# Feed-forward, block two: the final pair of row tiles also in seven products

## The chip, the core and the metric

The kernel runs on one core of a Trainium2 chip. The metric is the device time of one execution in microseconds. Five engines work side by side: TensorE (PE; its weight loads are PEld), VectorE (DVE), ScalarE (ACT), GpSimd (POOL) and SyncE (SP), which issues most loads. Each has its own list of instructions, fixed when the program is built, and engines wait for each other and for loads by semaphores.

## The reference

One decoder layer on 256 tokens of width 2048. The change touches the feed-forward at its end alone:

```python
h = x + jnp.concatenate([gla_out, nsa_out], axis=-1) @ w_out
m = rms_norm(h, ffn_norm_g)
return h + (jax.nn.silu(m @ w_gate) * (m @ w_up)) @ w_down
```

`w_gate` and `w_up` are 2048 x 5632, `w_down` is 5632 x 2048, all float32. What comes before (gated linear attention and native sparse attention) is not touched.

## The kernel before

**Blocks.** The 5632 hidden columns are cut into eleven blocks of 512, `fb` = 0 to 10; the change is in the second, `fb` = 1, called block two here. For each block `gate_up(fb)` makes gate and up for the 256 tokens (two token tiles of 128), and `down(fb - 1)` then multiplies the hidden values of the block before by 512 rows of `w_down` and adds them to the output. So after `gate_up(1)` comes `down(0)`, in four pieces `n` of 512 output columns, 24 matmuls each.

**Pairs.** The 2048 rows of the weights are 16 row tiles of 128, taken in 8 pairs. Plainly, a pair is eight products of a 128 x 128 token tile with a 128 x 512 weight tile (two row tiles, two token tiles, gate and up). In the other way, in the manner of Strassen and Winograd, it is seven products of sums of tokens with sums of weights. Each product is three matmuls (L1179), since float32 values are split into a high and a low part: 24 matmuls plainly, 21 with seven products. `FIRST7` and `PAIRS7` say which pairs of a block go in seven products; in block two they are 0, 2, 3, 4 and 5, and 1, 6 and 7 go plainly. The order of its pairs is `ORDER1 = (0,1,2,6,3,4,5,7)`, so pair 7 is last. The sums of tokens (`forms`) of pairs 6 and 7 are made by `late_forms` while block two runs, for the blocks after it.

**Splitting.** `in_parts` makes the high part with ScalarE (a copy that rounds, L661) and the low part with VectorE (what is left, L662). A plain pair splits its raw tile of four times 512 columns (`parts_of`). A pair of seven products splits three of the four (128 x 1536) and then two sums of 128 x 1024, `s1` and `s2` (`parts_of2`). The sums of some pairs were made early in the kernel and put into memory (`SUMS`, `sum_rows`); GpSimd's queue fetches them back (`fetch_sums`, L1168). For the others VectorE makes them when they are needed (L1210 to L1212), from the raw tile.

**Buffers.** Raw tiles come from SyncE's queue (`load4`, L1138) into three buffers `fraw`; split tiles lie in four buffers `ftwo`. A buffer is written anew when its last reader is done.

**Banks.** The products of a block are added up in eight PSUM banks, `banks[1]` to `banks[8]`. In the order lists below bank 1 is `bank_4463`, bank 2 `bank_4349`, bank 3 `bank_4368`, bank 4 `bank_4385`, bank 5 `bank_4478`, bank 6 `bank_4486`, bank 7 `bank_4482` and bank 8 `bank_4397`. Seven products of a pair add into banks 1 to 7, a plain pair adds into 2, 3, 4 and 8. So after the last pair of seven products (`last7`) banks 1, 5, 6 and 7 are final. They are read there (L1237 to L1241) into `q1`, `u`, `q5u`, `q7u` and `q57u`, and in block two three things follow from this point: `turn_act(0, (1, 5))` may transpose the hidden values of block one through banks 1 and 5, and `seed(0, ...)` puts the output's first piece into banks 6 and 7 (L1291), on which `down(0)` begins. With `last7` = 5 all this is issued ahead of pair 7; after pair 7 follow banks 2, 3, 4 and 8 with the silu and the product of gate and up (L1252 to L1256).

**Order.** The code gives the order in which instructions are issued; a scheduler moves them within each engine's list when the program is built, and the lists below are what it made.

Of the kernel before, what the change touches and what calls it, by code (L numbers as in the profile page):

```python
# [37 lines left out]
def kernel(  # L38
# [986 lines left out]

    PAIRS7, FIRST7 = tuple(range(8)), {0: (0, 2, 4), 1: (0, 2, 3, 4, 5)}

    EARLY7 = (0,1,2,3,4,5)  # L1030

# [414 lines left out]
```

## Time and profile before

| | |
|---|---|
| median of 3 runs | 1099.7 us (1098.82 to 1100.81) |
| the profiled execution | 1100.68 us |
| its span, first to last instruction | 1098.9 us |
| TensorE's granted clock | 1.000 |
| the first down stage, after block two | 495.39 to 517.22 us of the span |
| weights loaded and sums written and fetched, over the span | 271.22 MB, mean 247 GB/s |

Busy time of TensorE is partly modelled, so holes in it are seen best as waits of its weight loads (PEld) and in the chain of work that ended last. "Idle before" of a row, in square brackets, names what released it.

### The profile page before, as it was taken

How to read it: one execution, taken by the hardware profiler on the slowest of the kernel's cores; microseconds unless marked ns; L12 is line 12 of the kernel's file. 1: busy time of each engine (PE TensorE's matmuls, PEld its weight loads, DVE VectorE, ACT ScalarE, POOL GpSimd, SP SyncE). 2: the span in 40 equal slices, each digit the busy share in tenths (PEclk: the TensorE clock that was granted, in tenths of full speed). 3: DMA queues.
4: the chain of work that ended last, by engine and by line, in shares of the span. 5: the costliest groups of instructions: out<-in, count | busy, mean ns of one | idle time of the engine just before them, and what ended most of it. 6: DMA issues, size and time to landing. Idle time of an engine off the chain costs nothing.

```text
span 1098.9 us, 14699 instructions
## 1 busy us (share of the span) xinstructions
PE 1092.1 (99%) x5274; PEld 899.8 (82%) x5274; DVE 993.4 (90%) x1313; ACT 755.4 (69%) x1048; POOL 79.8 (7%) x150
## 2 busy tenths in 40 slices
PE   9999999999999999999999999999999999999998
PEld 8888888987888877888878888888888888888887
DVE  5778879986899888997999999999999999999997
ACT  7755557545687587666585866768585867777785
POOL 4100001032110100100000000000000000000000
PEclk9999999999999999999999999999999999999999
DMA  7999978467877956685566657576566768677663
GB/s 278 356 371 355 378 248 296 165 226 283 307 276 253 336 183 232 226 324 172 181 231 210 213 199 252 180 253 208 209 230 205 252 216 287 212 263 235 226 230 115
DMA packets 128885, 271.22 MB, mean 247 GB/s; under 512 B 7126, under 2 KB 9210, under 8 KB 128812
## 3 DMA queue, kind: packets, MB, share of 16 engines
q1 hardware_dynamic: 115532, 223.68, 59.2%
q0 software_dynamic: 12672, 46.14, 11.4%
q8 instruction: 41, 0.67, 0.2%
q10 hardware_dynamic: 608, 0.47, 0.1%
q14 instruction: 32, 0.26, 0.1%
HBM read 247.19 MB, written 23.07 MB: 246 GB/s over the span
## 4 chain that ended last, share of the span: by engine, by line
PE 82%; DVE 8%; issue 4%; ACT 3%; POOL 2%; DMA 1%; SPq 0%; DVEq 0%; POOLq 0%; ACTq 0%
PE bank L297 39%; PE bank L1179 36%; PE bank L215 2%; PE bank L1320 2%; DVE lo L145 2%; DVE ftwo L662 1%; DMA g<-in_x_dram 1%; PE bank L977 1%; ACT hi L144 1%; POOL sm L218 1%; DMA fraw<-in_w_up_dram 1%; ACT g L912 1%; DVE g L1111 0%; DVE g L1210 0%; POOL sc L218 0%
## 5 line engine op out<-in xcount | busy, mean ns | idle before, releaser
L1179 PE MATMUL bank<-ftwo,g 128*128 128x512 f32 x1842 | 431.3, 393 | 0.5 <-ACT ftwo L661 0.2
L1179 PEld LDWEIGHTS bank<-ftwo,g 128*128 128x128 f32 x1842 | 341.0, 188 | 77.9 <-DVE ftwo L662 5.0
L297 PE MATMUL bank<-hi,g 128*128 128x512 f32 (+1 forms) x1088 | 320.9, 376 | 0.4 <-ACT g L912 0.4
L662 DVE TENSOR_TENSOR ftwo<-fraw,ftwo 128x1536 fp32r<-128x1536 f32 (+1 forms) x130 | 256.6, 1976 | 8.2 <-ACT ftwo L661 7.4
L661 ACT ACTIVATE ftwo<-fraw 128x1536 fp32r<-128x1536 f32 (+1 forms) x130 | 216.0, 1664 | 28.3 <-DMA fraw<-in_w_up_dram 18.6
L297 PE MATMUL bank<-ftwo,g 128*128 128x512 f32 x960 | 220.6, 390 | 0.0
L297 PEld LDWEIGHTS bank<-hi,g 128*128 128x128 f32 x1088 | 191.6, 188 | 30.9 <-issue 1.0
L297 PEld LDWEIGHTS bank<-ftwo,g 128*128 128x128 f32 x960 | 179.6, 188 | 38.4 <-ACT bank L1291 0.3
L297 PE MATMUL bank<-lo,g 128*128 128x512 f32 (+3 forms) x544 | 193.0, 375 | 0.1
L144 ACT ACTIVATE hi<-raw 128x1024 fp32r<-128x1024 f32 (+3 forms) x124 | 130.7, 1059 | 81.9 <-PE bank L297 62.7
L145 DVE TENSOR_TENSOR lo<-raw,hi 128x1024 fp32r<-128x1024 f32 (+3 forms) x124 | 150.2, 1218 | 33.5 <-ACT hi L144 32.9
L661 ACT ACTIVATE ftwo<-g 128x1024 fp32r<-128x1024 f32 x76 | 80.3, 1057 | 75.1 <-DVE g L1210 48.9
L297 PEld LDWEIGHTS bank<-lo,g 128*128 128x128 f32 x544 | 98.3, 189 | 14.6 <-DVE lo L145 0.3
L662 DVE TENSOR_TENSOR ftwo<-g,ftwo 128x1024 fp32r<-128x1024 f32 x76 | 92.7, 1220 | 10.5 <-ACT ftwo L661 10.5
L662 DVE TENSOR_TENSOR ftwo<-fsum,ftwo 128x1024 fp32r<-128x1024 f32 x76 | 92.6, 1219 | 0.5 <-ACT ftwo L661 0.5
L661 ACT ACTIVATE ftwo<-fsum 128x1024 fp32r<-128x1024 f32 x76 | 79.6, 1048 | 5.4 <-DVE fsum L1212 3.7
L1303 ACT COPY g<-bank 128x512 f32<-128x512 f32 x80 | 46.0, 589 | 38.3 <-PE bank L297 36.7
L1210 DVE TENSOR_TENSOR g<-fraw 128x1024 f32<-128x1024 f32 x54 | 65.2, 1219 | 0.8 <-DMA fraw<-in_w_up_dram 0.8
L1291 ACT COPY bank<-g 128x512 f32<-128x512 f32 x80 | 45.3, 594 | 15.0 <-DVE f L1240 8.4
L661 ACT ACTIVATE g<-bank 128x512 fp32r<-128x512 f32 x46 | 27.2, 598 | 30.2 <-PE bank L215 24.3
L1168 POOL DMA_DIRECT2D g<-sums x20 | 10.6, 533 | 502.0 <-DVE ftwo L662 473.4
L215 PE MATMUL bank<-ident,g 128*128 128x128 f32 (+3 forms) x232 | 42.8, 278 | 1.3 <-DVE g L863 0.9
(250 smaller groups left out, 918.5 us busy)
## 6 DMA issues: line engine op xcount, KB each, us to landing
fraw<-in_w_gate_dram SPq DMA_DIRECT2D x86, 512.0 KB, 3.9
fraw<-in_w_down_dram SPq DMA_DIRECT2D x42, 1024.0 KB, 5.0
raw<-in_w_in_dram SPq DMA_DIRECT2D x36, 1024.0 KB, 5.8
fraw<-in_w_up_dram SPq DMA_DIRECT2D x66, 512.0 KB, 4.8
sums<-g POOLq DMA_DIRECT2D x40, 512.0 KB, 6.5
raw<-in_w_out_dram SPq DMA_DIRECT2D x16, 1024.0 KB, 8.6
g<-in_w_gate_dram SPq DMA_DIRECT2D x20, 512.0 KB, 8.4
g<-in_w_up_dram SPq DMA_DIRECT2D x20, 512.0 KB, 9.3
```

The lines of the kernel that those rows point to most:

```text
L144: act(h[:, i:i + n], r[:, k + i:k + i + n], AF.Copy)
L145: last["d"] = TT(o[:, i:i + n], r[:, k + i:k + i + n], f32(h[:, i:i + n]), ALU.subtract)
L215: return nc.tensor.transpose(o, i, ident[:n, :n])
L218: nc.gpsimd.tensor_tensor(o, i, mhalf[:i.shape[0], :i.shape[1]], ALU.pow)
L297: last["mm"] = mm(bk[t], a[:, k, t * P:(t + 1) * P], ws[k][m][:, off:off + w], start=(first_ and k == 0 and i == 0), stop=(end and k == 3 ...
L661: act(hi, ps, AF.Copy)
L662: last["d"] = TT(lo, ps, f32(hi), ALU.subtract)
L1179: mm(banks[q], x, m, start=todo[q] == total[q], stop=todo[q] == 1)
L1210: TT(s1, r[:, 1:3], r[:, 3:4].to_broadcast([P, 2, 512]), ALU.add)
L1291: last["seed", n] = nc.scalar.copy(banks[qs[n][t]], h_sb[n][:, t, :])
L1303: nc.scalar.copy(h_sb[n][:, t, :], bs[t])
L1320: mm(bk, u, m, start=(first and i == 0), stop=(end and i == 2), skip_group_check=onto)
```

## The change

Pair 7 joins the seven-product pairs of block two:

```diff
@@ FIRST7 @@
-    PAIRS7, FIRST7 = tuple(range(8)), {0: (0, 2, 4), 1: (0, 2, 3, 4, 5)}
+    PAIRS7, FIRST7 = tuple(range(8)), {0: (0, 2, 4), 1: (0, 2, 3, 4, 5, 7)}
```

`SUMS[1]` stays `(2, 3, 4, 5)`, so no sums of this pair lie in memory and VectorE makes them. `last7` of block two becomes 7, so the reads of banks 1, 5, 6 and 7, the transposes and the seeds are issued after pair 7, not ahead of it. Pair 7 is the last of its order and takes its products as 6, 1, 5, 7, 2, 3, 4; the scheduler puts 1, 5, 7, 2 and two matmuls of 3 first, then one of 6, one of 3, one of 4, the four transposes into bank 1, and the remaining two of 6 and of 4. No load is added or taken away, and the lists of the later blocks have the same order as before, but for a few VectorE rows of the next block's first two pairs.

On VectorE, where pair 4 of block two is split (`ftwo_4855` holds the sums of pair 3, `fraw_4876` is the raw tile of pair 4, `ftwo_4891` holds its sums, `fraw_4940` is the raw tile of pair 7), before and with the change as one difference:

```order
 L662 TENSOR_TENSOR ftwo_4855<-g_873_4802,ftwo_4855 128x1024 [waits DMASW6_49,Activation_49]
+L1210 TENSOR_TENSOR g_892_4946<-fraw_4940 128x1024 [waits DMAHW7_49,DMAHW0_49]
 L662 TENSOR_TENSOR ftwo_4879<-fraw_4876,ftwo_4879 128x1536 [waits DMAHW4_49,DMAHW3_49,Activation_49]
 L662 TENSOR_TENSOR ftwo_4891<-g_877_4836,ftwo_4891 128x1024 [waits DMASW7_49,Activation_49]
 L662 TENSOR_TENSOR ftwo_4891<-fsum_4837,ftwo_4891 128x1024 [waits DMASW5_49,Activation_49]
```

The first sum of pair 7 is new in VectorE's list, two pairs early, and it waits for both loads of that pair's raw tile.

On VectorE at the end of block two, before (`ftwo_4955` is pair 7, `ftwo_5006` and `ftwo_5041` are the first two tiles of `w_down`):

```order
L662 TENSOR_TENSOR ftwo_4955<-fraw_4952,ftwo_4955 128x2048 [waits DMAHW7_49,DMAHW0_49,Activation_49]
L662 TENSOR_TENSOR ftwo_5006<-fraw_5004,ftwo_5006 128x2048 [waits DMAHW1_49,Activation_49]
L1238 TENSOR_TENSOR f_891_4941<-bank_4486,f_890_4940 128x512 [waits PE_49,Activation_49]
L662 TENSOR_TENSOR ftwo_5041<-fraw_5039,ftwo_5041 128x2048 [waits DMAHW2_49,Activation_49]
L1239 TENSOR_TENSOR f_892_4942<-bank_4478,f_891_4941 128x512 [waits DVE_49]
L1240 TENSOR_TENSOR f_893_4943<-bank_4482,f_891_4941 128x512
L1252 TENSOR_TENSOR f_890_4940<-bank_4349,f_890_4940 128x512 [waits PE_49]
L1241 TENSOR_TENSOR f_894_4944<-bank_4478,f_893_4943 128x512 [waits DVE_49]
```

and with the change (`ftwo_4943` is the raw tile of pair 7, `ftwo_4951` its two sums, `ftwo_5013`, `ftwo_5048` and `ftwo_5079` are the first three tiles of `w_down`, `g_901` the low part of the hidden values of block one):

```order
L662 TENSOR_TENSOR ftwo_4943<-fraw_4940,ftwo_4943 128x1536 [waits Activation_49]
L1211 TENSOR_TENSOR fsum_4947<-g_892_4946,fraw_4940 128x512 [waits DVE_49]
L662 TENSOR_TENSOR ftwo_4951<-g_892_4946,ftwo_4951 128x1024 [waits Activation_49]
L1212 TENSOR_TENSOR fsum_4947<-fsum_4947,fraw_4940 128x512 [waits DVE_49]
L662 TENSOR_TENSOR ftwo_5013<-fraw_5011,ftwo_5013 128x2048 [waits DMAHW1_49,Activation_49]
L662 TENSOR_TENSOR ftwo_5048<-fraw_5046,ftwo_5048 128x2048 [waits DMAHW2_49,Activation_49]
L662 TENSOR_TENSOR ftwo_4951<-fsum_4947,ftwo_4951 128x1024 [waits Activation_49]
L662 TENSOR_TENSOR g_901_4998<-bank_4463,g_900_4997 128x4x128 [waits Activation_49]
L1238 TENSOR_TENSOR f_896_4978<-bank_4486,f_895_4977 128x512 [waits PE_49]
L662 TENSOR_TENSOR ftwo_5079<-fraw_5077,ftwo_5079 128x2048 [waits DMAHW3_49,Activation_49]
L1239 TENSOR_TENSOR f_897_4979<-bank_4478,f_896_4978 128x512 [waits DVE_49]
L1240 TENSOR_TENSOR f_898_4980<-bank_4482,f_896_4978 128x512
```

The second sums of pair 7 are split behind two tiles of `w_down`, and of the reads of banks 6, 5 and 7 the first stands behind them, the others behind a third such tile.

On ScalarE at the same place, before:

```order
L661 ACTIVATE ftwo_4955<-fraw_4952 128x2048 [waits DMAHW0_49,DMAHW7_49,DVE_49,PE_49]
L661 ACTIVATE ftwo_5006<-fraw_5004 128x2048 [waits DMAHW1_49,DVE_49,PE_49]
L1237 ACTIVATE f_890_4940<-bank_4463 128x512 [waits PE_49]
L661 ACTIVATE ftwo_5041<-fraw_5039 128x2048 [waits DMAHW2_49,DVE_49,PE_49]
L1291 COPY bank_4486<-g_540_3045 128x512 [waits DVE_49]
L661 ACTIVATE ftwo_5072<-fraw_5070 128x2048 [waits DMAHW3_49,PE_49,Activation_49]
```

and with the change:

```order
L661 ACTIVATE ftwo_4943<-fraw_4940 128x1536 [waits DMAHW0_49,DMAHW7_49,DVE_49,PE_49]
L661 ACTIVATE ftwo_4951<-g_892_4946 128x1024 [waits DVE_49,PE_49]
L661 ACTIVATE ftwo_5013<-fraw_5011 128x2048 [waits DMAHW1_49,DVE_49,PE_49]
L661 ACTIVATE ftwo_5048<-fraw_5046 128x2048 [waits DMAHW2_49,DVE_49,PE_49]
L661 ACTIVATE ftwo_4951<-fsum_4947 128x1024 [waits DVE_49]
L1237 ACTIVATE f_895_4977<-bank_4463 128x512 [waits PE_49]
L661 ACTIVATE g_900_4997<-bank_4463 128x4x128 [waits PE_49]
L661 ACTIVATE ftwo_5079<-fraw_5077 128x2048 [waits DMAHW3_49,Activation_49]
L1291 COPY bank_4486<-g_540_3045 128x512 [waits DVE_49]
L661 ACTIVATE ftwo_5112<-fraw_5110 128x2048 [waits DMAHW4_49,PE_49,Activation_49]
```

The seed of bank 6 (L1291 into `bank_4486`) stood behind two tiles of `w_down`; now it stands behind three, behind the split of the transposed hidden values (`g_900`) and behind pair 7's sums.

## The prediction

> **What bounds the kernel now.** I read the page's totals first, then the chain of work that ended last in order of time, then the stretches around the end of block two (the code's `fb = 1`), and last the timeline, row by row.
>
> ```profile
> PE 1092.1 (99%) x5274; PEld 899.8 (82%) x5274; DVE 993.4 (90%) x1313; ACT 755.4 (69%) x1048; POOL 79.8 (7%) x150
> PE 82%; DVE 8%; issue 4%; ACT 3%; POOL 2%; DMA 1%; SPq 0%; DVEq 0%; POOLq 0%; ACTq 0%
> ```
>
> TensorE carries 82% of the chain, VectorE 8%. The chain in order of time (start, length) says where:
>
> ```profile
> 423.71 68.72 PE bank L1179 x300
> 492.42 0.22 PE bank L215 x2
> ...
> 494.95 0.44 PE bank L215 x4
> 495.39 21.83 PE bank L297 x96
> ...
> 587.26 32.90 PE bank L1179 x144
> ```
>
> From 423.71 to 517.22, the whole of block two and of the first down stage, TensorE runs without a hole. A gate/up matmul costs 68.72 / 300 = 0.229 us, one of the down stage 21.83 / 96 = 0.227; eight transposes take 0.88. So a saved matmul is worth 0.229 us, and every hole in TensorE's stream is paid in full. By 587 it runs full again, so nothing later has room to give a loss back.
>
> ```profile
> 470.00:480.00 10.00, 10.00 (x45) 8.27 (x45) 8.81 (x8) 6.92 (x7) 0.53 (x1) 1.00 1.02 381
> 480.00:490.00 10.00, 10.00 (x46) 8.26 (x45) 8.55 (x7) 8.27 (x7) 0.00 (x0) 1.00 0.68 234
> 510.00:520.00 10.00, 10.00 (x46) 8.26 (x45) 4.58 (x5) 5.91 (x8) 0.00 (x0) 1.00 0.63 205
> ```
>
> The columns are sum, PE, PEld, DVE, ACT, POOL, granted clock, DMA share and GB/s. In the 20 us ahead of the block's end VectorE is idle for only 1.19 + 1.45 = 2.6 us, and the DMA engines are full (1.02) from 470 to 480.
>
> **What goes and what comes.** Pair 7 falls from 24 matmuls to 21: 3 x 0.229 = 0.69 us less on TensorE. VectorE's prices, by shape:
>
> ```profile
> L662 DVE TENSOR_TENSOR ftwo<-fraw,ftwo 128x2048 fp32r<-128x2048 f32 x12 | 27.3, 2286 | 1.0 <-ACT ftwo L661 1.0
> L662 DVE TENSOR_TENSOR ftwo<-fraw,ftwo 128x1536 fp32r<-128x1536 f32 x12 | 21.1, 1756 | 3.8 <-ACT ftwo L661 3.5
> L662 DVE TENSOR_TENSOR ftwo<-fsum,ftwo 128x1024 fp32r<-128x1024 f32 x12 | 14.6, 1219 | 0.0
> L1210 DVE TENSOR_TENSOR g<-fraw 128x1024 f32<-128x1024 f32 x7 | 8.4, 1219 | 0.0
> L1211 DVE TENSOR_TENSOR fsum<-g,fraw 128x512 f32<-128x512 f32 x7 | 4.7, 686 | 0.1
> ```
>
> In a full queue starts are some 0.08 us closer than these lengths (1.14 us between 480.63 and 481.77 below): 0.60, 1.14, 1.67 and 2.20 us by size. Out goes one subtraction of 2048 (2.20); in come L1210 (1.14), L1211 and L1212 (0.60 each), a subtraction of 1536 (1.67) and two of 1024 (1.14 each): 6.29 - 2.20 = 4.1 us more, where 2.6 us are idle. ScalarE gets 1536 more elements, under 2 us, and waits for others there. No load is added; the sums of pair 7 never go through memory.
>
> **The first hole: a load at the head of VectorE's queue.** L1210 now stands ahead of the subtraction of pair 4's raw tile and waits for both loads of pair 7.
>
> ```profile
> 467.79 0.37 SPq L1138 DMA_DIRECT2D fraw<-in_w_gate_dram  x1
> 468.20 0.47 SPq L1138 DMA_DIRECT2D fraw<-in_w_up_dram  x1
> 470.03 0.37 SPq L1138 DMA_DIRECT2D fraw<-in_w_gate_dram  x1
> 470.44 0.52 SPq L1138 DMA_DIRECT2D fraw<-in_w_up_dram  x1
> ...
> 471.86 1.22 DVE L662 TENSOR_TENSOR ftwo<-g,ftwo 128x1024 fp32r<-128x1024 f32 x1
> 473.23 1.76 DVE L662 TENSOR_TENSOR ftwo<-fraw,ftwo 128x1536 fp32r<-128x1536 f32 x1
> 480.63 1.23 DVE L662 TENSOR_TENSOR ftwo<-g,ftwo 128x1024 fp32r<-128x1024 f32 x1 [0.48 <-ACT ftwo L661]
> 481.77 1.22 DVE L662 TENSOR_TENSOR ftwo<-fsum,ftwo 128x1024 fp32r<-128x1024 f32 x1
> 481.58 1.92 ACT L661 ACTIVATE ftwo<-fraw 128x2048 fp32r<-128x2048 f32 x1
> ```
>
> VectorE is at L1210's place at 473.0 (the end of the 471.86 row); the subtraction behind it ran at 473.23. Pair 7's loads were issued at 470.03 and 470.44, and no row gives their landing: nobody waited for them. I bound it by what SP's queue (q1) moved from 467.8 to 478.0 and from 467.8 to 479.0:
>
> ```profile
> q1 hardware_dynamic: 921, 1.77, 47.7%
> q1 hardware_dynamic: 1095, 2.11, 51.8%
> fraw<-in_w_down_dram SPq DMA_DIRECT2D x4, 1024.0 KB, 5.1
> ```
>
> Pair 5's loads (512 and 256 KB) and pair 7's (1024 KB) are 1.84 MB. q1 had moved 1.77 MB at 478.0 and 2.11 at 479.0, so in order the last byte passes near 478.2 at the earliest; the latest is 481.58, where ScalarE began on the tile. The w_down tile queued behind already has a share of q1's bytes, so I take 479.3, an estimate nearer the early end.
>
> Pair 4 starts on TensorE 57 matmuls (21 + 21 + 15) before 492.42, at 479.37. Its first matmul needs only the hi part and ends at 479.60; the second needs the subtraction. That now ends at 479.3 + 1.14 + 1.75 = 482.2: **hole 1, 2.6 us**. Before, it was done at 475.0.
>
> Does VectorE really wait in order?
>
> ```profile
> 508.84 0.37 SPq L1138 DMA_DIRECT2D fraw<-in_w_gate_dram  x1
> ...
> 513.87 1.76 DVE L662 TENSOR_TENSOR ftwo<-fraw,ftwo 128x1536 fp32r<-128x1536 f32 x1 [2.22 <-ACT ftwo L661]
> 518.82 1.23 DVE L662 TENSOR_TENSOR ftwo<-g,ftwo 128x1024 fp32r<-128x1024 f32 x1 [3.20 <-ACT ftwo L661]
> 523.42 2.35 DVE L1210 TENSOR_TENSOR g<-fraw 128x1024 f32<-128x1024 f32 x2
> ```
>
> It sat idle for 3.20 us up to 518.82, with an L1210 queued whose load was issued ten us before. The Trainium skill says the same in its page Perfetto Trace Analysis, section Tensor Engine Instruction: "ACT/DVE/GPSIMD are strict FIFO"; by that rule hole 1 stands and the sum is 7.0, by an engine that took pair 4's subtraction first it would be the 3.2 of the first rival.
>
> **The end of the block.** VectorE is full from 479.3 on. In the new order, adding up: pair 4 done 484.4, pair 5 done 488.3, pair 7 raw 490.0, L1211 and the first sums' subtraction 491.8, L1212 492.4, the first two w_down tiles 496.8, and only then the subtraction of pair 7's second sums, done 498.0. TensorE: 482.2 + 20 and 21 matmuls puts pair 7's start at 491.6; 17 matmuls and four transposes later, at 495.95, it needs those second sums: **hole 2, 2.0 us**. Four matmuls end the pair at 498.9.
>
> ```profile
> 484.30 1.92 ACT L661 ACTIVATE ftwo<-fraw 128x2048 fp32r<-128x2048 f32 x1 [0.80 <-PE bank L1179]
> 489.18 0.59 ACT L1291 COPY bank<-g 128x512 f32<-128x512 f32 x1 [0.68 <-DVE f L1238]
> ```
>
> The down stage starts in bank 6, which must be read (L1238) and seeded (L1291) first. Before, the seed ran at 489.18, six us ahead of its use, because pair 7 did not touch bank 6. Now bank 6 ends at 498.5, and ahead of the seed ScalarE splits the third w_down tile, whose buffer comes free with L1212 at 492.4; 5.1 us of load make that 497.6, the split ends at 499.5, the seed at 500.0: **hole 3, 1.1 us**. Twelve matmuls on, at 502.8, the second four transposes need bank 5, last read by L1241, which stands behind that third tile's subtraction (499.5 + 2.2) and three more reads: 504.3, **hole 4, 1.5 us**. The next matmuls wait for bank 2's seed, behind a copy, a seed and a silu on ScalarE: **hole 5, 0.4 us**.
>
> Sum: 2.6 + 2.0 + 1.1 + 1.5 + 0.4 - 0.7 = **+7.0 us** (unrounded 7.01). What is behind is covered: at the next block's start VectorE had waits of 2.22 and 3.20 us for work that TensorE's progress released; those move with TensorE and take up the 4.1 us.
>
> The profiled execution took 1100.68 us, 1.8 over its span; with the sum 1107.7. The median shown is 1.0 below that execution: **1106.7 us**.
>
> **Rivals.**
> - *The load is in time, the end of the block is not.* If pair 7 lands by 475, as 4.8 us after issue would give, hole 1 is gone. Holes 2 to 5 stay at 1.1, 1.0, 1.4 and 0.4, since VectorE's subtraction of the second w_down tile then waits for a buffer that pair 5's last matmul frees at 488.99: +3.2, 1102.9 us. q1's bytes speak against it. Chance 0.14.
> - *Not slower.* The one mechanism: pair 7's second sums are subtracted before TensorE asks for them, 17 matmuls and four transposes after 488.99, so by 493.3, and the bank reads follow at once. Then only the 0.69 counts: 1099.0 us. It needs the load by 475 and some 1.1 us less in VectorE's queue ahead of that row; for it speaks the 2.6 us of idle time, against it the two w_down subtractions queued ahead. Chance 0.08.
> - *A longer first hole.* With landing at 481.5 hole 1 is 4.8 us: +9.2, 1108.9 us. If TensorE's clock also fell to half for the 20 matmuls that pair 4 has left, they would cost 20 x 0.229 = 4.6 us more: 1113.5. Chance 0.07 in all.
>
> ```profile
> 553.06 4.73 PEld L1179 LDWEIGHTS bank<-ftwo,g 128*128 128x128 f32 x21 [0.53 <-DVE ftwo L662]
> ```
>
> The longest hole before in these blocks is this 0.53 us, and the granted clock stays 1.00. The Trainium skill, TensorE: Matmul & The Clock Gate, section What's actually happening, has the clock halved after an idle window of about 3.4 us; by that rule a hole of 2.6 leaves it alone and one of 4.8 may not, and no row here can show it. That the change does not do what it says is excluded by the instruction lists: three matmuls fewer, five VectorE instructions more.
>
> **How the numbers follow.** My forecast has 0.71. The landing's ends, 478.2 and 481.58, give +5.9 and +9.2; the first rival +3.2. The range runs from 1102.4, just under the first rival, to 1109.2 and leaves out the second rival and the clock. A measurement of this kernel tells 0.2% (2.2 us) from no change: slower 0.91, same 0.07, faster 0.02.
>
> **What would show it.** In the profile after: VectorE idle from 473 to about 479 ahead of an L1210 released by a load from w_up; a wait of some 2.6 us of TensorE's weight loads for a VectorE L662 near 479.6; three shorter waits between 495 and 505, for L662, for an L1291 and for an L1241; 96 down matmuls ending near 524.2 instead of 517.2; everything after as before, 7 us later. I am wrong if L1210 starts near 475, or if the seed of bank 6 is ready when pair 7 ends.

## The result and the profile after

The changed kernel took **1109.9 us** (median of 4 runs, 1109.4 to 1110.49), the kernel before in the same session 1099.26 us (4 runs, 1098.19 to 1100.81): a ratio of 1.0098, 95% interval 1.0083 to 1.0113. That is 10.6 us slower; 7.0 had been forecast, and the time lies 0.7 us above the range. Its profiled execution took 1109.87 us, its span is 1108.1 us, its granted clock 0.997.

The page's totals and its chain by engine, to set beside those of before:

```profile
PE 1095.0 (99%) x5271; PEld 901.3 (81%) x5271; DVE 997.5 (90%) x1318; ACT 757.1 (68%) x1050; POOL 79.6 (7%) x150
PE 79%; DVE 9%; issue 4%; ACT 4%; DMA 3%; POOL 1%; SPq 0%; DVEq 0%; ACTq 0%; POOLq 0%
```

Three matmuls fewer and five VectorE instructions more, as the change says. TensorE nevertheless counts 2.9 us more of busy time: matmuls have become slower somewhere. The chain (start, length) shows where, from the start of the block to the end of the first down stage:

```profile
423.12 29.28 PE bank L1179 x126
...
469.84 9.09 DMA fraw<-in_w_up_dram
...
480.09 1.76 DVE ftwo L662
481.90 11.23 PE bank L1179 x41
493.15 1.93 ACT ftwo L661
495.10 3.44 DVE ftwo L662 x2
...
500.71 3.07 PE bank L297 x12
...
506.13 20.95 PE bank L297 x84
```

Before, TensorE held this stretch alone; now it is taken in turns by a load, VectorE, ScalarE and TensorE. TensorE's own timeline (start, length, idle before and its releaser) names five holes:

```profile
481.90 15.13 PE L1179 MATMUL bank<-ftwo,g 128*128 128x512 f32 x58 [2.77 <-DVE ftwo L662]
...
498.58 1.19 PE L1179 MATMUL bank<-ftwo,g 128*128 128x512 f32 x4 [1.11 <-DVE ftwo L662]
500.71 3.06 PE L297 MATMUL bank<-ftwo,g 128*128 128x512 f32 x12 [0.94 <-ACT bank L1291]
504.69 0.66 PE L215 MATMUL bank<-ident,f 128*128 128x128 f32 x4 [0.92 <-DVE f L1241]
506.13 2.32 PE L297 MATMUL bank<-ftwo,g 128*128 128x512 f32 x6 [0.79 <-ACT bank L1291]
```

And VectorE ahead of the first of them:

```profile
471.26 1.22 DVE L662 TENSOR_TENSOR ftwo<-g,ftwo 128x1024 fp32r<-128x1024 f32 x1
478.95 1.22 DVE L1210 TENSOR_TENSOR g<-fraw 128x1024 f32<-128x1024 f32 x1 [6.47 <-DMA fraw<-in_w_up_dram]
```

VectorE was free from 472.5 on, and its next row, the subtraction of pair 4 that hole 1 waits for, begins at 480.09, when the sum is made. All five holes are where they were forecast and in their order. Four also have the reason that was given; hole 3 has not quite. The row that released it is not the split of the third `w_down` tile on ScalarE but, 0.13 us later, VectorE's read of bank 6 (L1238), which itself waited for TensorE:

```profile
498.00 1.91 ACT L661 ACTIVATE ftwo<-fraw 128x2048 fp32r<-128x2048 f32 x1
499.35 0.69 DVE L1238 TENSOR_TENSOR f<-bank,f 128x512 f32<-128x512 f32 x1 [0.22 <-PE bank L1179]
500.07 0.59 ACT L1291 COPY bank<-g 128x512 f32<-128x512 f32 x1 [0.17 <-DVE f L1238]
```

What was not forecast stands in TensorE's granted clock. The rows below are windows of 3.41 us (their columns: window, length, TensorE busy and its matmuls, granted clock, DMA share, GB/s):

```profile
479.55:482.96 3.41, 1.06 (x5) 1.00 0.07 4
482.96:486.37 3.41, 3.41 (x10) 0.50 0.89 303
496.61:500.03 3.42, 2.05 (x10) 1.00 1.04 388
500.03:503.44 3.41, 2.73 (x12) 1.00 0.61 226
503.44:506.85 3.41, 1.71 (x9) 1.00 0.87 300
506.85:510.27 3.42, 3.42 (x10) 0.50 0.03 5
```

Twice the clock is 0.50 for exactly one such window. The count of such a window is 10 matmuls, those that its borders cut included, where a full window at full clock counts 17. Each of the two follows a window in which TensorE was busy for half the time or less.

**The account.** TensorE needed 527.08 - 423.12 = 103.96 us for this stretch, and 517.22 - 423.71 = 93.51 before: 10.45 more. Of that, -0.69 are the three matmuls saved; two windows at half clock lose 3.41 / 2 = 1.7 us each, 3.4 together; 7.7 are left for the holes, 6.5 of them idle time in the rows above (2.77 + 1.11 + 0.94 + 0.92 + 0.79) and the remaining 1.2 fit what is lost at their edges, where matmuls no longer overlap (the four at 498.58 take 1.19 us, not 4 x 0.229 = 0.92). Outside this stretch the profile after is shorter by 0.59 us ahead of it and by 0.66 us behind it.

### The profile page after: what moved, and what is told of

The parts are those of the page before. It is cut to its first block, busy times and chain, and to the rows that moved or that the text cites. A ratio compares the mean times of both kernels' runs of the same rounds, so it can differ in the third digit from the quotient of the medians.

```text
span 1108.1 us, 14704 instructions
## 1 busy us (share of the span) xinstructions
PE 1095.0 (99%) x5271; PEld 901.3 (81%) x5271; DVE 997.5 (90%) x1318; ACT 757.1 (68%) x1050; POOL 79.6 (7%) x150
## 4 chain that ended last, share of the span: by engine, by line
PE 79%; DVE 9%; issue 4%; ACT 4%; DMA 3%; POOL 1%; SPq 0%; DVEq 0%; ACTq 0%; POOLq 0%
PE bank L297 39%; PE bank L1179 33%; PE bank L215 2%; DVE ftwo L662 2%; PE bank L1320 2%; DVE lo L145 1%; DMA fraw<-in_w_up_dram 1%; DMA g<-in_w_up_dram 1%; PE bank L977 1%; ACT hi L144 1%; POOL sm L218 1%; DMA sums<-g 1%; ACT g L912 1%; ACT ftwo L661 1%; DVE g L1111 0%
## 5 line engine op out<-in xcount | busy, mean ns | idle before, releaser
L662 DVE TENSOR_TENSOR ftwo<-fraw,ftwo 128x1536 fp32r<-128x1536 f32 (+1 forms) x130 | 255.9, 1969 | 8.6 <-ACT ftwo L661 7.9
L662 DVE TENSOR_TENSOR ftwo<-g,ftwo 128x1024 fp32r<-128x1024 f32 x77 | 93.8, 1218 | 9.4 <-ACT ftwo L661 9.4
L662 DVE TENSOR_TENSOR ftwo<-fsum,ftwo 128x1024 fp32r<-128x1024 f32 x77 | 93.7, 1217 | 1.0 <-ACT ftwo L661 1.0
L1210 DVE TENSOR_TENSOR g<-fraw 128x1024 f32<-128x1024 f32 x55 | 66.3, 1216 | 6.5 <-DMA fraw<-in_w_up_dram 6.5
L1291 ACT COPY bank<-g 128x512 f32<-128x512 f32 x80 | 45.3, 593 | 14.4 <-DVE f L1240 8.6
L1168 POOL DMA_DIRECT2D g<-sums x20 | 10.6, 531 | 512.3 <-DVE ftwo L662 483.7
```

The costliest lines, as they stand in the source:

```text
L662: last["d"] = TT(lo, ps, f32(hi), ALU.subtract)
L1210: TT(s1, r[:, 1:3], r[:, 3:4].to_broadcast([P, 2, 512]), ALU.add)
L1291: last["seed", n] = nc.scalar.copy(banks[qs[n][t]], h_sb[n][:, t, :])
```

## The experiments

The theory after the result: VectorE's place in line for pair 7's load (hole 1) and the late bank reads and seeds (holes 2 to 5) cost what was forecast, and holes close together also halve the clock. The rivals: the extra sums cost VectorE's queue wherever they stand; or the place of pair 7 as the last pair costs; or the clock has nothing to do with the holes. Each was timed in five rounds beside the kernel before. That took 1099.39 us (median of 17 runs) beside the sum put behind, the sum alone, pair 6 last and the early sums; 1099.51 (15) beside pair 7 in the middle, the first seed ahead and the unused additions; 1098.67 (17) beside the sum alone again, that sum later and the changed kernel once more.

### The sum behind the last addition on VectorE

```diff
-                    TT(s1, r[:, 1:3], r[:, 3:4].to_broadcast([P, 2, 512]), ALU.add)
+                    with behind(last["d"] if fb == 1 else None):
+                        TT(s1, r[:, 1:3], r[:, 3:4].to_broadcast([P, 2, 512]), ALU.add)
```

> The change, but the first sum of pair 7 (L1210, here L1211) is tied behind the subtraction of pair 7's own raw tile, so VectorE no longer waits for that load ahead of pair 4. Theory (a load at the head of VectorE's queue opens the first hole, the shift of the bank reads behind pair 7 opens the others, and the clock halves for 3.4 us after TensorE has been idle for about half of such a stretch): no wait for L662 near 479, holes of 2 to 3 us in all between 489 and 503, granted clock 1.000 or one half-clock stretch at most (0.998), time 2 to 4 us above the kernel before. Rival (the 4.1 us of extra VectorE work are what costs, wherever L1210 stands): still 7 us or more above the kernel before, since the work is all there.

Measured: 1101.47 us (11 runs, 1100.62 to 1103.48), ratio 1.002 [1.0011, 1.0028]; clock 0.998 to 1.0. TensorE's waits in block two and its down stage:

```profile
PE bank L297 <- ACT bank L1292: 2.4, 2, 2.0
```

and the window at the block's end in which TensorE was busy least:

```profile
493.07:496.48 3.41, 1.98 (x9) 1.00 0.92 301
```

Hole 1 is gone, and with it 8.4 us of the change's 10.6, although its length is only some 3 us. What stays is the late seed, 2.0 + 0.4 us. Holes 2 and 4 are gone with hole 1, and so is the half clock in the profiled run, where even a window with 1.98 us of TensorE has full clock behind it. Only the two slowest of the eleven runs, 1102.7 and 1103.48 us, are at 0.998.

### The same sum alone, in the kernel before

The sum of pair 7's raw tile is made in the kernel before, at the same place in VectorE's queue, and nobody reads it.

```diff
+            if fb == 1 and pair == 7:
+                spare = g4([2, 512])
+                TT(spare, r[:, 1:3], r[:, 3:4].to_broadcast([P, 2, 512]), ALU.add)
```

> The kernel before, pair 7 plain in 24 matmuls, with one VectorE addition more: the first sum of pair 7's raw tile, made and read by nobody; it stands ahead of pair 4's subtraction as in the changed kernel. Theory: the first hole alone, 2.8 us, and one half-clock stretch of 3.4 us (1.7 us): 4.5 us above the kernel before, granted clock 0.998. Rival one (the clock fell for another reason than the hole): 2.8 us above, clock 1.000. Rival two (extra VectorE work costs by its length): 1.1 us above at most.

Measured: 1104.2 us (5 runs, 1102.86 to 1105.03), ratio 1.0042 [1.0029, 1.0055]; clock 1.0 in three runs and 0.998 in two. VectorE, TensorE and the windows of the profiled run, one of those at clock 1.0:

```profile
478.63 1.23 DVE L1206 TENSOR_TENSOR g<-fraw 128x1024 f32<-128x1024 f32 x1 [6.46 <-DMA fraw<-in_w_up_dram]
```

```profile
481.58 4.64 PE L1179 MATMUL bank<-ftwo,g 128*128 128x512 f32 x19 [2.76 <-DVE ftwo L662]
```

```profile
476.88:480.30 3.42, 1.95 (x9) 1.00 0.11 42
480.30:483.71 3.41, 2.13 (x9) 1.00 0.24 50
483.71:487.12 3.41, 3.41 (x17) 1.00 0.77 274
```

One added instruction that waits 6.46 us for a load costs 4.8 us in all. Its hole is as long as hole 1 of the changed kernel (2.76 and 2.77 us), but here the border of two windows cuts it into 1.46 and 1.28 us, and the clock stays full. So in this run the cost is not the clock's. TensorE's time from the start of block two (422.82) to the end of the first down stage (520.74) is 97.92 us, 4.4 more than in the profile before. Of that 2.76 are the hole, and 0.24 and 0.36 two later waits, at 497.39 and 499.12; the rest fits what is lost at the edges of the three: in the stream a matmul lasts 0.39 us and the next starts after 0.23, and this overlap is missing at a hole, where the first matmul behind it also lasts longer, 0.50 us. A late VectorE thus goes on costing at the block's end.

### That sum again, and the same sum later in the queue

The first is the same kernel once more, the second puts the unused sum behind the last addition on VectorE.

```diff
-                TT(spare, r[:, 1:3], r[:, 3:4].to_broadcast([P, 2, 512]), ALU.add)
+                with behind(last["d"]):
+                    TT(spare, r[:, 1:3], r[:, 3:4].to_broadcast([P, 2, 512]), ALU.add)
```

> The kernel before with the one unused sum of pair 7, once more (1104.2 us as run before; the hole was 2.76 us, cut into 1.46 and 1.28 us by the border of two windows, without half clock). Theory: the hole is 2.5 to 3 us again; where one window takes more than about 1.6 us of it, the next one has half clock and the time is 1.7 us more, so the granted clock is 1.0 in some runs and 0.998 in others, 1103 to 1105.5 us. Rival: the clock is the same in all runs.

> The kernel before with the same unused sum, but put behind the last addition on VectorE, so that it stands behind the subtractions of pairs 4 and 5, ahead of pair 7's own split, instead of ahead of pair 4's. Theory (its place in VectorE's queue costs, not its work): it no longer waits for the load, 1.15 us of VectorE lie ahead of pair 7's subtraction where TensorE has 4.6 us of work in hand; no hole at pair 4, clock 1.0, 1099.0 to 1100.4 us. Rival (one more sum of raw tiles costs VectorE's queue that much wherever it stands): 1101.5 us or more.

Measured, the kernel again: 1104.26 us (6 runs, 1102.61 to 1106.36), ratio 1.0049 [1.0036, 1.0061]. Its three runs at clock 1.0 took 1102.61, 1103.13 and 1103.79 us, two at 0.998 took 1104.73 and 1104.79, one at 0.997 took 1106.36. The profiled run is of 0.998; in it the hole of 2.51 us lies within one window:

```profile
479.03:482.44 3.41, 0.95 (x4) 0.99 0.00 0
482.44:485.85 3.41, 3.41 (x10) 0.51 0.93 298
```

So the same kernel has the half-clock window in some runs and not in others, by where its hole falls on the windows; the medians of the two groups (all three runs below 1.0 in one) differ by 1104.79 - 1103.13 = 1.7 us. The five runs of the first time separate less: 1102.86, 1103.87 and 1105.03 us at 1.0, 1104.2 and 1104.22 at 0.998. The groups are small; that a half-clock window costs 1.7 us rests on its length, 3.41 us at half the rate.

Measured, the sum later: **1099.31 us** (11 runs, 1098.72 to 1100.51), ratio 1.0006 [0.9997, 1.0014], clock 1.0 in every run. VectorE's rows there:

```profile
480.76 1.22 DVE L662 TENSOR_TENSOR ftwo<-fsum,ftwo 128x1024 fp32r<-128x1024 f32 x1
481.89 1.22 DVE L1207 TENSOR_TENSOR g<-fraw 128x1024 f32<-128x1024 f32 x1
483.03 4.50 DVE L662 TENSOR_TENSOR ftwo<-fraw,ftwo 128x2048 fp32r<-128x2048 f32 x2
```

The same 1.22 us of work, six places later, waits for nothing and costs nothing that can be measured. The place costs, not the work: the rival of an addition that costs wherever it stands is out for this one sum.

### Pair 6 last

The row order of the middle blocks is changed so that the plain pair 6 covers the bank reads, with the sum behind as above.

```diff
-    ORDER1 = (0,1,2,6,3,4,5,7)
+    ORDER1 = (0,1,2,3,4,5,7,6)
```

> The change with pair 7 ahead of pair 6 (order 0, 1, 2, 3, 4, 5, 7, 6) and its first sum tied behind its own raw tile: the plain pair 6, 24 matmuls, stands between the last pair of seven products and the down stage again. The same products, sums and matmuls as the change. Theory: no hole over 0.6 us and clock 1.000; what is left is 3 matmuls saved, 0.7 us below the kernel before, and at most 1 us above it if VectorE's 4.1 us of extra work are not all covered. Rival (extra VectorE work costs wherever it stands): 3 us or more above.

Measured: 1122.46 us (4 runs), ratio 1.0206 [1.0193, 1.0219]. A miss, and mostly of the edit: seven blocks use this order, so it moved pairs in all of them. TensorE's waits over the whole span:

```profile
PE bank L1179 <- ACT ftwo L661: 12.1, 20, 1.1
```

The 12.1 us for ScalarE's splits come in 20 pieces, only 1.4 us of them in block two. But block two's own down stage misses the forecast too: a wait of 2.9 us for VectorE's `w_down` subtractions (L662) ends at 501.06, and with the waits ahead of it a window holds 1.42 us of TensorE, with two at half clock behind it. So the cover of pair 6 did not clear the block's end here. As a test of the place alone it says little, since the later blocks are changed as well; the next run but one repeats it for block two alone.

### Pair 7's sums made early and fetched

```diff
-    SUMS[1] = (2, 3, 4, 5)
+    SUMS[1] = (2, 3, 4, 5, 7)
```

> The change, but the sums of pair 7 of block two are made early in the kernel and fetched from memory, as those of its other pairs (SUMS[1] gets 7), so that VectorE makes none here; pair 7 stays last. Theory: no first hole, clock 1.000; the bank reads and the seed still stand behind pair 7, so holes of 0.5 to 2.5 us in all stay between 489 and 503: 0 to 2 us above the kernel before. Rival (the wait for the load is only moved to another instruction): a hole of over 2 us near 479 stays and the time is 4 us or more above.

Measured: 1105.72 us (6 runs, 1104.46 to 1110.03), ratio 1.0064 [1.0049, 1.0079], clock 0.998 in all six. TensorE's waits from 360 us to the end of the first down stage:

```profile
PE bank L297 <- ACT g L661: 2.4, 1, 2.4
PE bank L215 <- ACT g L1075: 1.8, 1, 1.8
```

Hole 1 is gone here too, with no sum of pair 7 left to VectorE. But the bank reads still stand behind pair 7 with nothing to cover them (2.4 us at 497.28, and a half-clock window behind it), and there is a hole near 380 us (1.8), where early sums are made, that the kernel before does not have. The forecast, 0 to 2 us above the kernel before, was too low by 4. Two of the six runs, 1108.48 and 1110.03 us, lie 3 us and more above the profiled one at the same clock; why, no trace shows.

### Pair 7 in the middle of block two

```diff
+        if fb == 1:
+            order = (0, 1, 2, 3, 7, 4, 5, 6)
         last7 = max(sevens, key=order.index)
```

> The changed kernel with block two's order of row tiles alone set to 0, 1, 2, 3, 7, 4, 5, 6: pair 7 stays in seven products but stands fifth, the plain pair 6 is last, and the sum of its raw tiles is put behind the last addition on VectorE. The bank reads then come after pair 5 as before, with pair 6's 24 matmuls behind them as cover. Theory (what costs is the place of pair 7, not its sums): none of the five holes, full clock, 1098.5 to 1100.5 us, since 0.7 us of matmuls are saved and pair 7's two extra splits take places where VectorE has about 4.6 us of slack. Rival (the seventh product's sums cost VectorE's queue wherever they stand): a wait for VectorE in the middle of the block, 1102 us or more.

Measured: 1101.62 us (11 runs, 1099.69 to 1102.97), ratio 1.0019 [1.001, 1.0028]. Neither theory nor rival in full: nothing waits in the middle of the block, yet three short waits remain at its end, the third of 0.3 us beside these two, and one of 0.8 us comes in the next block, at 547.76:

```profile
PE bank L297 <- ACT g L661: 0.8, 1, 0.8
PE bank L297 <- ACT bank L1294: 0.4, 1, 0.4
```

With pair 7's own sums in the rotation of the buffers of sums, ScalarE now waits for the fetched sums of pair 5 until they land, and everything behind them in its queue is later:

```profile
483.28 1.06 ACT L661 ACTIVATE ftwo<-fsum 128x1024 fp32r<-128x1024 f32 x1 [1.43 <-DMA fsum<-sums]
```

So even with cover behind it pair 7 in seven products does not pay here. That it is the rotation that delays the fetch was not tried apart.

### The first seed ahead of the third tile's split

On top of the sum put behind, ScalarE's split of the third `w_down` tile stands behind the first seed, as in later stages.

```diff
-last["seed", 0] if n == 2 and f else None
+last["seed", 0] if n == 2 else None
```

> The changed kernel with the sum behind the last addition (1101.5 us as run before) and one more edit: in the first down stage the third weight tile's split stands behind the first seed on ScalarE, as it does in later stages. Theory (the 2.0 us that TensorE still waits for a seed of bank 6 come from that split, 1.7 to 1.9 us on ScalarE ahead of the seeds): that wait falls to 0 to 0.7 us, and the time to 1099.4 to 1100.5 us. Rival (the seed is late because its bank is read late by VectorE, so its place in ScalarE's queue is nothing): 1101 to 1102 us, the wait still 2 us.

Measured: 1103.88 us (5 runs, 1102.81 to 1104.71), ratio 1.0042 [1.003, 1.0055], clock 0.998 in every run: 2.4 us worse, not 1 to 2 better. ScalarE:

```profile
494.84 0.59 ACT L1292 COPY bank<-g 128x512 f32<-128x512 f32 x1 [1.32 <-DVE f L1239]
...
497.16 1.91 ACT L661 ACTIVATE ftwo<-fraw 128x2048 fp32r<-128x2048 f32 x1
```

The rival is right for most of the wait: the seed now waits for VectorE's read of bank 6 (L1239 there), which comes behind a `w_down` subtraction, and TensorE's wait only falls from 2.04 to 1.67 us. Those 0.4 us were the split's: before this edit it ended at 493.96, 0.5 after the read. The time fits neither forecast. The split, moved back, now delays the hidden values that TensorE needs next, and a window with 1.55 us of TensorE halves the clock:

```profile
498.18:501.60 3.42, 1.55 (x9) 1.00 0.12 47
501.60:505.01 3.41, 3.41 (x9) 0.50 0.02 5
```

### Five and eight unused additions

In the kernel before, additions of 1024 elements on data that is long there; eight in the second.

```diff
+            if fb == 1 and pair == 7:
+                spare = g4([2, 512])
+                for _ in range(5):
+                    TT(spare, h_sb[0], h_sb[0], ALU.add)
```

> The kernel before with five unused additions of 1024 elements (1.14 us each) put on VectorE in block two, ahead of the split of pair 7's weights, all on data that are long there. The earlier unused sum held VectorE for 6.46 us of waiting and 1.14 us of work and left a hole of 2.76 us, so the slack is 4.84 us; five additions take 5.7 us, the hole should be 0.9 us. Theory (the clock halves for 3.4 us, at a cost of 1.7 us, after a window of 3.4 us in which TensorE was busy for less than about half): no half clock in any run, 1099.8 to 1101 us. Rival (any hole of about 1 us can halve it): some runs at clock 0.998 and 1102 us or more.

> The kernel before with eight such additions at the same place: 9.1 us on VectorE less the slack of 4.84 us makes a hole of about 4.3 us. Theory (a window of 3.4 us less than about half busy halves the clock, and windows run freely): a hole longer than such a window halves the clock once in every run, some runs twice; 1099.4 + 4.3 + 1.7 = 1105.4 us, range 1104.5 to 1107.5, granted clock 0.998 or lower in every run. Rival (the half clock of the changed kernel had nothing to do with the holes): clock 1.0 and 1103.0 to 1104.0 us.

Measured: 1105.0 us (5 runs, 1104.52 to 1107.23) and 1109.0 us (5 runs, 1108.33 to 1109.66), ratios 1.0057 [1.0044, 1.0069] and 1.0089 [1.0075, 1.0103]; clocks 0.997 to 0.998 and 0.995 to 0.997. Both miss, since the scheduler spread the additions from 470 to 495 us, in part among the bank reads. With five, the hole came there and was 2.66 us, not 0.9; it left 1.16 us of TensorE in one window, and half clock followed. The longest hole with eight:

```profile
502.52 5.84 PE L297 MATMUL bank<-ftwo,g 128*128 128x512 f32 x18 [4.20 <-DVE ftwo L662]
```

What holds is the part on the clock: with a hole of 4.20 us, longer than a window, every run is below 1.0. There, two windows in a row at half clock follow one with 0.92 us of work:

```profile
495.53:498.94 3.41, 0.92 (x2) 0.99 0.00 0
498.94:502.35 3.41, 0.00 (x0) 0.50 0.00 0
502.35:505.77 3.42, 3.25 (x8) 0.51 0.55 195
```

The place fits the +5.5: at the block's end an addition costs about its full time (three more took 4.0 us more, 3 x 1.22 = 3.7 of them work), while the single unused sum that stood ahead of those reads cost nothing. How the cost of five parts between the additions and the half window was not tried apart.

### The changed kernel once more

> The changed kernel as it is, once more, for a second profile whose clock windows lie elsewhere against the program. Theory (windows of 3.41 us run freely; after a window in which TensorE's busy time is 1.71 us or less the next one has half clock, after one of 1.95 us or more it has not): holes of 2.8 us at pair 4 and of 1.1, 0.9, 0.9 and 0.8 us at the block's end as before, and each window of half clock follows a window of that grid with 1.9 us or less of TensorE; no window with less is left without one. Granted clock 0.997 (two such windows) in most runs, 1109 to 1111 us. Rival (the clock falls for another reason): a window of half clock behind a busy one, or none behind an idle one.

Measured: 1110.88 us (5 runs), ratio 1.0108 [1.0095, 1.0121]. Clock and time of the runs: 0.998 and 1108.33; 0.996 and 1109.8; 0.995 and 1110.88, 1111.94 and 1112.2. The profiled run, at 0.995, has three windows at half clock:

```profile
494.26:497.67 3.41, 1.59 (x10) 1.00 1.04 380
497.67:501.08 3.41, 2.86 (x8) 0.50 1.02 357
501.08:504.50 3.42, 3.42 (x10) 0.50 0.89 299
504.50:507.91 3.41, 1.49 (x9) 1.00 0.28 108
507.91:511.32 3.41, 3.41 (x10) 0.50 0.02 5
```

and none behind its first hole, 2.67 us long, which the border of two windows cuts:

```profile
477.19:480.60 3.41, 1.67 (x8) 1.00 0.05 17
480.60:484.02 3.42, 2.50 (x11) 1.00 0.35 111
```

The half windows again follow idle ones, at other holes than in the first profile. The holes themselves are not the same either: 2.67, 1.82, 0.55 and 1.92 us, and none ahead of the second four transposes (hole 4). Two more points of the expectation fail. A window with 1.67 us of TensorE has none behind it, so the busy time alone does not draw the line between 1.59 and 1.95 us (with 1.71, four of its nine instructions transposes, one followed). And the second of the two half windows in a row follows one with 2.86 us, itself at half clock: there, 8 matmuls of half speed were not enough to come back, while windows filled to 3.4 us were, and so was the one of 3.25 above and one of 2.99 with five additions.

## Why the prediction was wrong, and where it was right

**The load (right).** Pair 7's landing was estimated at 479.3; VectorE began at 478.95 in an execution that reached block two 0.59 us earlier (423.12 against 423.71), so 479.5 on the clock of before. The bounds from the bytes of SyncE's queue were enough for a landing that no row gave.

**Strict order on VectorE (right).** Pair 4's subtraction stood ready and waited behind L1210. The unused sum shows it alone: 4.8 and 5.6 us ahead of that subtraction, 0.6 us with an interval from -0.3 to 1.5 us behind it. The Trainium skill's rule cited from Perfetto Trace Analysis, section Tensor Engine Instruction, agrees with these runs.

**The five holes (right in kind and nearly in sum, the latter partly by luck).** Forecast 2.6, 2.0, 1.1, 1.5 and 0.4, together 7.6; found 2.77, 1.11, 0.94, 0.92 and 0.79 of idle time, together 6.5, and 7.7 only with what was lost at their edges, which the sum did not have. Holes 2 and 4 are shorter than forecast, hole 5 is longer, and the second profile has no hole 4. For hole 2 that fits the first half-clock window, which brought TensorE to it 1.7 us later; in the second profile, where that window is missing, the same hole is 1.82 us. For hole 3 the prediction put ScalarE's split last; in the profile VectorE's read of bank 6 came last, by 0.13 us, and with the sum put behind it was the split, by 0.5.

**What follows (right, but 10 us later and not 7).** Nothing was given back or lost by much: the rest of the span took 1108.1 - 527.08 = 581.0 us after and 1098.9 - 517.22 = 581.7 before.

**The clock (wrong: this step failed).** The prediction gave a longer first hole and a halved clock a chance of 0.07 together and said that by the rule of an idle window "a hole of 2.6 leaves it alone". It judged one hole against the length of a window. The runs show windows on a fixed grid, each judged by how busy TensorE was in it: 2.77 us of hole left 1.06 us of work in one window of the first profile, and the holes of 0.92 and 0.79 us left 1.71 in another. A series of short holes counts like a long one. Each half window costs 1.7 us; the profiled run had two, so the term that the sum lacked is **3.4 us**. As the hole behind the first of them shrank (1.11 us where the second profile has 1.82), what both added in the end may be less, by up to some 0.7. The times of the second session agree: about 1.6 us apart per window (1108.33 with one by its clock, 1110.88 to 1112.2 with three), which leads back to some 1106.7 with none, a case that no run showed.

The Trainium skill's page TensorE: Matmul & The Clock Gate, section What's actually happening, says that the window of 3413 ns runs freely; the grid of windows and the different place of its borders from run to run agree with it. Its words on re-throttling after an idle window of 3.4 us do not fit as they stand: windows that were 31% and 50% busy were followed by half clock.

**The step to the median (off by 1.0).** The sum was set 1.0 us below its profiled value, since the profiled execution of before stood that far above its median. That of after stands on its median. With it the miss closes in the books: 3.4 (clock) + 0.1 (holes) - 0.59 - 0.66 + 1.0 = 3.25, where 1109.9 - 1106.7 = 3.2.

**The rivals.** The load in time and the kernel not slower did not happen. A longer first hole did not either; only the half clock that was tied to it did. The signs chosen to tell right from wrong came out as forecast but for the end of the 96 down matmuls, 527.1 instead of 524.2, and what hangs on it; that is where the clock shows.

**What remains without hole 1.** The sum put behind leaves 2.1 us over the kernel before, pair 7 in the middle 2.1, early sums 6.3. No variant with pair 7 in seven products was faster than the kernel before: in each, the waits that came with it took more than the 0.69 us saved. That the late reads and splits alone are the cause was not tried apart.

## What to carry to other kernels

An instruction that waits for a load belongs behind everything on its in-order engine that is already ready: here one such sum cost 4.8 us in all at one place and nothing measurable six places later. On a stream of matmuls without holes, a forecast of holes needs a second term for the clock: lay windows of 3.41 us over the stretch, at any offset, and where one can come out about half busy or less, add 1.7 us. A few matmuls saved count only if the waits that come with them are smaller: here 0.69 us were saved, and with the seventh product of pair 7 last or in the middle 2.1 us were lost.

## What the runs showed of the hardware that was not expected

- Half clock comes in whole windows of 3.41 us. After a window at full clock with 1.59 us of TensorE or less the next one was at half clock; after one with 1.95 us or more none was. Between them 1.71 was followed by half clock, and 1.67 and 1.74 (early sums, the window from 378.93) were not.
- The border of the windows lies elsewhere in each profiled execution. The hole of the unused sum, 2.51 and 2.76 us in its two profiles, cost a half window in five of eleven runs, by their granted clock, and none in the others: up to 1.7 us of scatter between runs of one kernel.
- A half-clock window that was itself 2.31 us (pair 6 last) or 2.86 us busy was followed by another; one of 2.99 (five additions) or 3.25 us was not.
- A hole costs TensorE more than its idle time: with the unused sum 3.4 us of idle time in three holes made the stretch 4.4 us longer at full clock. Matmuls that follow each other every 0.23 us last 0.39 us each, and at a hole this overlap is lost.
